# Retention's output projection as a one-level Strassen product in two parts of K

## The chip, the core and the metric

The kernel runs on one core of one Trainium2 chip. A core has a matrix engine (PE, TensorE), a vector engine (DVE), an activation engine (ACT), a general engine (POOL, GpSimd) and a queue that issues transfers (SP). Each engine carries out its own list of instructions in order and waits where an operand is not ready. The metric is the device time of one execution in microseconds. The median of three runs of the kernel before is 1336.56 us (1333.08 to 1337.13).

## The reference

One inference step of a two-layer trunk: a retention layer, then a sliding-window attention layer, for 1024 prompt tokens and 8 decode tokens of width 1024. What matters here is the end of the retention layer:

```python
    o, S = retention_scan(q, k, v, S0)
    o = rmsnorm(o, g_out.reshape(RET_HEADS, RET_DV)).reshape(B, L, RET_V)
    o = o * jax.nn.silu(gate)
    return x + o @ w_out, S.astype(S0.dtype)
```

There are 4 heads of 512 value columns, so `o` is tokens x 2048 and `w_out` is 2048 x 1024: the output projection has K = 2048, 1024 features and 1032 tokens. The attention layer then normalises the result `x + o @ w_out` and projects it to queries, keys, values and a gate. All values are float32.

## The kernel before

All projections are matmuls of 128x128 weights against up to 512 token columns. To keep float32 accuracy each operand is split into a rounded part ("hi", made by ACT or DVE) and a remainder ("lo", a subtraction on POOL or DVE), and each product is made of three matmuls: hi with hi, hi with lo, lo with hi.

The program has four stages on PE. *Input projection* (to about 546 us): q, k, v and the gate of the retention layer. Most of it is already a one-level Strassen product: `SEQ7` lists seven products of a weight combination (`A11`, `S1`, ...) with a token combination (`B11`, `T1`, ...), which take the place of eight. Its results go to DRAM. *Retention* (to about 700 us): 32 steps, each one chunk of 128 tokens of one head, heads 0 and 1 alternating through all 8 chunks, then heads 2 and 3. A step loads q, k, v and gate from DRAM, forms scores, updates the state, normalises, transposes the result to features x tokens (`b_tr`), multiplies it by the gate (`b_og`, DVE) and splits it: `b_oh` on ACT writes the hi part, `b_ol` on POOL (line 998) the lo part, into `A_hi`, `A_lo` (first 512 tokens) and `B_hi`, `B_lo` (the rest). *Output projection* (lines 1188 to 1190): for each of 8 feature tiles, 16 K tiles against 512 token columns, then again against 256 and 264. The first 24 matmuls (`e_mm`, lines 1026 to 1028) run before the last step's transposes. `wslot` loads and splits the weights 512 KB at a time, twice over, once for each half of the tokens. `ro_finish` adds the residual x by transposes into the same accumulator, writes the result to the DRAM buffer `xscr`, sums squares, and for the second half splits it at once into `A_hi`, `A_lo`; `reload2` brings the first half back. *Attention layer*: K/V projection (`kv_mm`, line 1338) from 901 us, then query and gate projections interleaved with attention (lines 1134 to 1136), then the last output projection.

In the input projection and the retention the order of every engine's work is written out by hand: PE has a list of slots, and the other engines' operations are placed by planned times or by slot (`when`, `later`) and then issued in that order. In the output projection PE's order is that of the loops, and the other engines' instructions are ordered by the compiler's scheduler.

## Time and profile before

| | us |
|---|---|
| median of three runs | 1336.56 |
| span of the profiled execution | 1336.3 |
| PE busy | 1293.8 (97%) |
| POOL busy | 832.5 (62%) |
| DVE busy | 743.8 (56%) |
| ACT busy | 668.4 (50%) |
| first matmul of the output projection | 700.49 |
| first matmul of the K/V projection | 901.01 |

Times in the profile are counted from the start of the profiled execution; its span is the profiled execution's own time, and lies 0.3 us under the median of the runs. A row of a timeline gives start, duration, engine, line, operation, output<-inputs and shape; in square brackets stands the idle time just before it and what ended that. PE's matmuls are pipelined: the duration of one is longer than its distance to the next, so costs are read from distances between starts. "PEclk" or "granted clock" is the share of PE's full clock that was granted.

### The profile page before, as it was taken

To read this page: it belongs to the slowest core of one execution; us is meant where nothing else is said; L and a number is where in the kernel's file an instruction comes from. 1 tells how busy PE (TensorE), PEld (TensorE's weight loads), DVE (VectorE), ACT (ScalarE), POOL (GpSimd) and SP (SyncE) were. 2 spreads that over 40 slices of the span, in tenths; PEclk is the share of its full clock that TensorE was granted. 3 is DMA by queue.
4 is the path that set the end of the run, shared out by engine and by line. 5 is a ranking of instruction groups with operands and counts; after the bars stand their busy time and mean duration, and the time that the engine had idled before them with its cause. 6 is when DMAs were issued, how large, how long until landed. Compare 5 with 4: busy or idle time off the path is not lost. (4 is left out here: it accounts for less than half of the span.)

```text
span 1336.3 us, 25984 instructions
## 1 busy us (share of the span) xinstructions
PE 1293.8 (97%) x9421; PEld 1233.6 (92%) x9421; DVE 743.8 (56%) x1497; ACT 668.4 (50%) x1692; POOL 832.5 (62%) x968
## 2 busy tenths in 40 slices
PE   6999999999999999898998999999999999999998
PEld 5999999999999999787886889999999999998998
DVE  6953665665565654477772212315677777778411
ACT  5532555555555653476771011235577666766321
POOL 6653556656556664398895654545688787868410
PEclk9999999999999999899998999999999999999999
DMA  6313767576666752656455634551131121103532
GB/s 223 103 58 118 241 189 248 157 243 213 195 211 215 231 174 83 191 161 218 158 165 164 188 110 136 155 151 47 58 95 48 33 60 33 48 20 116 176 95 76
DMA packets 193859, 187.18 MB, mean 140 GB/s; under 512 B 12756, under 2 KB 173580, under 8 KB 193716
## 3 DMA queue, kind: packets, MB, share of 16 engines
q1 hardware_dynamic: 160336, 153.19, 37.3%
q10 hardware_dynamic: 33396, 32.34, 7.7%
q8 instruction: 74, 1.21, 0.4%
q14 instruction: 53, 0.43, 0.1%
HBM read 129.11 MB, written 57.41 MB: 140 GB/s over the span
## 5 line engine op out<-in xcount | busy, mean ns | idle before, releaser
L340 PE MATMUL b<-xh,woh 128*128 128x258 f32 x784 | 222.2, 283 | 0.0
L342 PE MATMUL b<-xh,wol 128*128 128x258 f32 x784 | 221.7, 283 | 0.0
L341 PE MATMUL b<-xl,woh 128*128 128x258 f32 x784 | 221.4, 282 | 0.0
L1134 PE MATMUL pj<-A_hi,wh 128*128 128x384 f32 (+1 forms) x512 | 172.8, 337 | 0.0
L1135 PE MATMUL pj<-A_lo,wh 128*128 128x384 f32 (+1 forms) x512 | 164.6, 322 | 1.0 <-POOL A_lo L1489 0.7
L1136 PE MATMUL pj<-A_hi,wl 128*128 128x384 f32 (+1 forms) x512 | 164.3, 321 | 0.0
L340 PEld LDWEIGHTS b<-xh,woh 128*128 128x128 f32 x784 | 148.1, 189 | 1.2
L341 PEld LDWEIGHTS b<-xl,woh 128*128 128x128 f32 x784 | 148.7, 190 | 0.0
L342 PEld LDWEIGHTS b<-xh,wol 128*128 128x128 f32 x784 | 148.0, 189 | 0.0
L1124 POOL TENSOR_TENSOR wl<-wr,wh 128x1024 fp32r<-128x1024 f32 (+1 forms) x40 | 88.5, 2224 | 74.6 <-ACT wh L1121 37.8
L334 PE MATMUL b<-wol,xh 128*128 128x256 f32 x448 | 126.0, 281 | 1.2 <-DVE wol L224 1.2
L333 PE MATMUL b<-woh,xh 128*128 128x256 f32 x448 | 125.8, 281 | 0.0
L335 PE MATMUL b<-woh,xl 128*128 128x256 f32 x448 | 125.7, 281 | 0.0
L282 POOL TENSOR_TENSOR yl<-yd,yh 128x256 fp32r<-128x256 f32 x64 | 56.1, 876 | 79.6 <-PE od L289 40.3
L224 POOL TENSOR_TENSOR wol<-raw,woh 128x512 fp32r<-128x512 f32 x52 | 68.9, 1333 | 48.0 <-ACT woh L219 47.0
L1135 PEld LDWEIGHTS pj<-A_lo,wh 128*128 128x128 f32 x512 | 97.0, 189 | 1.6 <-POOL A_lo L1489 1.0
L1134 PEld LDWEIGHTS pj<-A_hi,wh 128*128 128x128 f32 x512 | 97.0, 189 | 0.6 <-issue 0.3
L1136 PEld LDWEIGHTS pj<-A_hi,wl 128*128 128x128 f32 x512 | 96.8, 189 | 0.0
L1688 POOL TENSOR_TENSOR s<-s,sm 128x512 f32<-128x512 f32 x64 | 66.6, 1040 | 34.0 <-DVE sm L1687 33.3
L334 PEld LDWEIGHTS b<-wol,xh 128*128 128x128 f32 x448 | 84.3, 188 | 1.4 <-DVE wol L224 1.4
L333 PEld LDWEIGHTS b<-woh,xh 128*128 128x128 f32 x448 | 84.3, 188 | 0.7
L335 PEld LDWEIGHTS b<-woh,xl 128*128 128x128 f32 x448 | 84.3, 188 | 0.0
(387 smaller groups left out, 3874.8 us busy)
## 6 DMA issues: line engine op xcount, KB each, us to landing
raw<-in_w_in_ret_dram ACTq DMA_DIRECT2D x44, 512.0 KB
st<-in_state_ret_dram SPq DMA_DIRECT2D x64, 256.0 KB
out_dram<-st SPq DMA_DIRECT2D x64, 256.0 KB
wr<-in_w_out_ret_dram SPq DMA_DIRECT2D x32, 512.0 KB
wr<-in_w_in_swa_dram SPq DMA_DIRECT2D x18, 512.0 KB
vb<-vscr SPq DMA_DIRECT2D x64, 128.0 KB
evp<-qks SPq DMA_DIRECT2D x32, 256.0 KB
evw<-gsc SPq DMA_DIRECT2D x32, 256.0 KB
```

The source lines that it names most:

```text
L224: eng.tensor_tensor(lo, src_of(s, name, sub), hi.bitcast(F32), SUB)
L333: mm(dst, xh, wh, start=a and i == 0, stop=False, skip_group_check=True)
L334: mm(dst, xh, wl, start=False, stop=False, skip_group_check=True)
L335: mm(dst, xl, wh, start=False, stop=z, skip_group_check=True)
L340: mm(dst, wh, xh, start=a, stop=False, **sg)
L341: mm(dst, wh, xl, start=False, stop=False, **sg)
L342: mm(dst, wl, xh, start=False, stop=z, **sg)
L1124: lo_eng[0].tensor_tensor(lo[:, js, :], raw[:, i:i + step, :], hi.bitcast(F32)[:, js, :], ALU.subtract)
L1134: mm(ps, hi[:, k, fs], xh[:, k, t0:t1], start=first and k == ks[0], stop=False)
L1135: mm(ps, hi[:, k, fs], xl[:, k, t0:t1], start=False, stop=False)
L1136: mm(ps, lo[:, k, fs], xh[:, k, t0:t1], start=False, stop=last and k == ks[-1])
L1688: nc.gpsimd.tensor_tensor(u.st[:, :, 0:256], u.st[:, :, 0:256], u.sm.unsqueeze(2).broadcast_to([128, 2, 256]), ALU.mult)
```

## The change

The output projection becomes a one-level Strassen product, made twice: once for the first half of K (heads 0 and 1) and once for the second (heads 2 and 3). Within a part, K is halved between the two heads, the features within a group of 256 are halved, and tokens are halved into even and odd chunks. There are 2 x 4 sets (part, group of 256 features), each of seven products in the order of `SEQ7`, each product in two slots (`t`, halves of the tokens) of 4 K tiles x 3 matmuls of 258 columns (256 prompt tokens and 2 decode tokens).

- Operands of part one: `b_og` writes the gated result of heads 0 and 1 into 16 held tiles (`hold`); `plan_builds` places the splits and the sums of five of the seven operands in steps 6 to 30 of the retention. The other two, T3 and T4, are split when the retention's tiles have been released (`late_build`). `b_oh`, `b_ol` and `e_mm` are gone.
- Operands of part two: `b_og` of heads 2 and 3 goes to DRAM (`osc`), is loaded again during sets 1 to 3 for the sums (`tsum`), stored, and all seven operands are loaded and split during the fourth set (`xb_load`, `xb_build`), through five buffers (`ob_load`).
- Partial results of part one, with the residual, go to DRAM (`pasc`), and are added in part two (`pa_load`, `pa_add`, `o_evac`). Weights are loaded once, and their sums formed on POOL (`w_sum`).
- The finished result goes to `xscr` and, except for the last 256 features, is loaded and split again (`a_load`, `a_split`) during the last set and at the start of the K/V projection, which now takes the odd chunks first (`KORD`).
- The whole kernel up to the last projection is now ordered by hand. The table `Table` has one slot of 1.45 us for each half product (0.23 more where residual transposes follow); its slots run from 0 to 169.8 us, the eight sets begin at 0, 22.1, 44.3, 66.4, 88.6, 108.9, 129.2 and 149.5, and the other engines' work is placed by these times.

The attention layer keeps its matmuls and their order after the K/V projection; its weight tiles are cut into pieces of another size.

```diff
+    osc = [dp.tile([8, 2, 128, 4, 128 + 2 * m], F32, name=f"osc{m}") for m in range(2)]
+    pasc = dp.tile([4, 4, 128, 516], F32, name="pasc")
...
-    A_hi = ap.tile([128, 8, NT], F32R, name="A_hi")
-    A_lo = ap.tile([128, 8, NT], F32R, name="A_lo")
-    A_hif = A_hi.bitcast(F32)
-    p2 = ExitStack()
-    bp = p2.enter_context(tc.tile_pool(name="bp", bufs=1, side="right", reuse_waits="tile"))
-    B_hi = bp.tile([128, 16, 520], F32R, name="B_hi")
-    B_lo = bp.tile([128, 16, 520], F32R, name="B_lo")
...
+    hold = {(h, c): ho.tile([128, 4, 128], F32, tag=f"h{h}{c}", name="hold") for h in range(2) for c in range(NCH)}
...
+    def xo_alloc(x):
+        pool_, n = (xb[0], 4) if x in (T3, T4) else (xo, 10)
+        OX[x] = [pool_.tile([128, 4, 2, 258], F32R, tag="xo", bufs=n, name=nm) for nm in ("oxh", "oxl")]
...
+    def ox_hi(x, j, src):
+        act(ox_cs(x, j, src.shape[2])[0], src, AF.Copy)
+
+    def ox_lo(x, j, src, eng=pool):
+        h, l = ox_cs(x, j, src.shape[2])
+        eng.tensor_tensor(l, src, h.bitcast(F32), SUB)
...
+        og = hold[h, c] if h < 2 else rp.tile([128, 4, 128], F32, name="og", bufs=2)
+        dve.tensor_tensor(og, d.pop(("pt", c)).rearrange("p (i t) -> p i t", i=4), d.pop(("g", c)), MUL)
+        if h >= 2:
+            ogs.append((osc[c // 2 % 2][(0, 2, 1, 3)[2 * (h % 2) + c % 2], c // 4][:, :, 0:128], og))
...
-    def e_mm():
-        ps = ro_ps[0, 0] = trp.tile([128, 512], F32, name="tr")
-        xh, xl, _ = o_view(0)
...
+    def plan_builds(first, last):
+        seq_ = []
+        for j in range(4):
+            a_, c_ = hold[0, 2 * j], hold[0, 2 * j + 1]
+            b_, d_ = hold[1, 2 * j], hold[1, 2 * j + 1]
+            for x, y in ((B11, a_), (B21, b_), (B22, d_)):
+                seq_ += [(ox_hi, x, j, y), (ox_lo, x, j, y)]
+            seq_ += [(sum_op, a_, c_, a_), (sum_op, c_, d_, c_), (ox_hi, T1, j, a_), (ox_lo, T1, j, a_),
+                     (sum_op, d_, d_, a_), (ox_hi, T2, j, d_), (ox_lo, T2, j, d_), (sum_op, b_, b_, d_)]
+        for n_, x in enumerate(seq_):
+            j = n_ * 4 // len(seq_)
+            builds.setdefault(max(4 * j + 6, first + n_ * (last - first) // len(seq_)), []).append(x)
+
+    plan_builds(6, 30)
...
+    def ob_load(n_, j):
+        y = ob[0].tile([128, 4, 128 + 2 * (j % 2)], F32, tag="ob", bufs=5, name="ob")
+        nc.sync.dma_start(out=y, in_=osc[j % 2][n_, j // 2])
+        return y
...
+    def o_product(s, ps, t, name, x, first, res):
+        hi, lo = s.op[name, 0]
+        dst = ps[:, 0:258]
+        for k in range(4):
+            wh, wl = hi[:, k, :], lo[:, k, :]
+            xh, xl = OX[x][0][:, k, t, :], OX[x][1][:, k, t, :]
+            a, z = first and k == 0, k == 3 and res is None
+            sg_k = dict(skip_group_check=not first)
+            mm(dst, wh, xh, start=a, stop=False, **sg_k)
+            mm(dst, wh, xl, start=False, stop=False, **sg_k)
+            mm(dst, wl, xh, start=False, stop=z, **sg_k)
+        if res is not None:
+            for i in range(2):
+                nc.tensor.matmul(ps[:, 128 * i:128 * i + 128], res[:, 2 * t + i, :], ident, is_transpose=True,
+                                 start=False, stop=(i == 1), skip_group_check=not first)
...
+    def o_raw(s, j):
+        t = s.pool().tile([128, 4, 256], F32, tag="raw", bufs=2, name="raw")
+        nc.sync.dma_start(out=t, in_=w_out_ret[1024 * s.part + 512 * j:1024 * s.part + 512 * j + 512, s.c0:s.c0 + 256]
+                          .rearrange("(k p) f -> p k f", p=128))
+        s.raw.append(t)
...
+        elif j == 3 and s.part == 0:
+            act(o_out(s, "c", t), b0, AF.Copy)
+        elif j == 3:
+            dve.tensor_tensor(o_out(s, "c", t), b0, s.pa["c"][:, t, :], ADD)
+        elif j == 4 and s.part and s.q:
+            dve.tensor_tensor(c["w", t], b1, c["w", t], ADD)
...
+    def out_a(s, key, i, par):
+        dc = both(s, key)[:, :, 256:258]
+        ft = 2 * s.q + i
+        pool.tensor_tensor(dc, dc, xd[:, ft, dsl(par)].rearrange("p (t c) -> p t c", t=2), ADD)
+        soon_dma(pasc[s.q, "cwxp".index(key)], s.full[key])
...
+        if s.q == 3:
+            if AT[3] is None:
+                at_alloc(3)
+            ahi, alo, af = [y[:, i, 0:NP].rearrange("p (t c r x) -> r p t c x", r=2, c=2, x=128)[par]
+                            for y in (*AT[3], AT[3][0].bitcast(F32))]
+            act(ahi, pr, AF.Copy, scale=gk)
+            dve.scalar_tensor_tensor(alo, pr, gk, af, MUL, SUB)
...
+    def a_split(k, par):
+        g = a_st.pop((k, par))
+        if AT[k // 2] is None:
+            at_alloc(k // 2)
+        gk = gcol[:, 16 + k:17 + k]
+        ahi, alo = [a_par(y[:, k % 2], par) for y in AT[k // 2]]
+        act(ahi, g, AF.Copy, scale=gk)
+        dve.scalar_tensor_tensor(alo, g, gk, ahi.bitcast(F32), MUL, SUB)
...
+        res = s.part == 0 and j >= 3
+
+        def pe():
+            if first:
+                s.bk[b, t] = o_bank(b, t)
+            o_product(s, s.bk[b, t], t, name, x, first, s.res[KEYS[j - 3][0]] if res else None)
+
+        tb.slot(1.45 + (0.23 if res else 0.0), pe)
+        tb.later(n + 1, o_evac, s, j, t)
...
+            th_ = max(tf - 6.5, floor + (3.2 if name != "A11" else 0.0))
+            tl_ = th_ + 1.4
...
+            tb.when(max(min(reads) - 15.0 + 0.5 * j, 10.0 if s is osets[1] else -1e9), o_raw, s, j)
...
+    def tsum(j):
+        a_, b_, c_, d_ = t_st.pop(j)
+        for eng, out, x, y, n_ in ((dve, a_, c_, a_, 4), (pool, c_, d_, c_, 6), (dve, d_, d_, a_, 5), (pool, b_, b_, d_, 7)):
+            eng.tensor_tensor(out, x, y, SUB)
+            soon_dma(osc[j % 2][n_, j // 2], out, 2)
...
+    def xb_build(x, j):
+        y = x_st.pop((x, j))
+        if j == 0:
+            xo_alloc(x)
+        ox_hi(x, j, y)
+        ox_lo(x, j, y, (dve, pool)[j % 2])
...
+    for n_, (x, j) in enumerate([(x, j) for x in (T3, T4) for j in range(4)]):
+        tb.when(4.5 + 0.6 * n_, late_build, x, j)
...
+        tb.when(13.0 + 12.3 * j, tsum_load, j)
+        tb.when(19.5 + 12.3 * j, tsum, j)
+    m = 0.0
+    for n_, x in enumerate(ORD7):
+        for j in range(4):
+            m = max(m + 1.1, osets[3].t0 + 2.95 * n_ + 3.0)
+            tb.when(m - 6.0, xb_load, x, j)
+            tb.when(m, xb_build, x, j)
...
+    for k in range(6):
+        m = e7 + 3.1 + 2.0 * k
+        tb.when(m - 5.0, a_load, k, 1)
+        tb.when(m, a_split, k, 1)
+    for k in range(2):
+        tb.when(e7 + 11.0 + k, a_load, k, 0)
+        tb.when(e7 + 15.6 + 2.0 * k, a_split, k, 0)
...
+    tb.pe()
+    others(len(steps))
+    store_s()
+    tb.rest()
+    for _ in range(2):
+        tb.pe()
+        if tb.n == 2:
+            at_step(b_tr, len(steps) - 1)
+        tb.rest()
+    others(len(steps) + 1)
+    store_s()
+    open_b()
...
-    npool = 0
-    for ft in range(8):
-        if ft:
-            drain(ro_part(ft, 0, 0, ps2 if npool % 3 else pjp))
-        npool += 1
-        drain(ro_part(ft, 0, 1, None))
-        ro_finish(ft, 0)
...
+    KORD = (1, 3, 5, 7, 0, 2, 4, 6, 8)
...
+    for k in range(2, 6):
+        a_load(k, 0, lambda: atp.tile([128, 4, 128], F32, tag="qs", bufs=4, name="ar"))
...
```

The order of the instructions shows the change at three places. First PE at the end of the retention. Before, the last early matmuls of the projection (`eh`, `el`: early weights) are followed by the transposes of the last step (`on`) and by the rest of the first tile (`wh`, `wl`: weights from `wslot`):

```order
L1028 MATMUL tr_9799<-A_hi_7711,el_7723 128x512
L1026 MATMUL tr_9799<-A_hi_7711,eh_7722 128x512
L1027 MATMUL tr_9799<-A_lo_7712,eh_7722 128x512
L1028 MATMUL tr_9799<-A_hi_7711,el_7723 128x512
L103 MATMUL tr_9824<-ident_69,on_9789 128x128 x4
L1188 MATMUL tr_9799<-A_hi_7711,wh_9860 128x512
L1189 MATMUL tr_9799<-A_lo_7712,wh_9860 128x512
L1190 MATMUL tr_9799<-A_hi_7711,wl_9861 128x512
```

Now the same transposes stand inside the second product (`oxh`, `oxl`: a token operand, `woh`, `wol`: a weight operand, `S`: an accumulator that held the state), between its two halves:

```order
L1127 MATMUL S_9885<-oxh_7739,woh_9818 128x258
L1128 MATMUL S_9885<-oxl_7740,woh_9818 128x258
L1129 MATMUL S_9885<-oxh_7739,wol_9819 128x258
L104 MATMUL tr_9898<-ident_71,on_9856 128x128 x4
L1127 MATMUL S_9919<-oxh_7739,woh_9818 128x258
L1128 MATMUL S_9919<-oxl_7740,woh_9818 128x258
L1129 MATMUL S_9919<-oxh_7739,wol_9819 128x258
```

The matmuls that stood ahead of the last transposes needed two 256 KB weight tiles; three slots of products stand there now.

Second, ACT in the middle of the projection. Before, it has the evacuation of a tile (`x`), its square and its store:

```order
L1213 ACTIVATE x_10070<-pj 128x256
L1213 ACTIVATE x_10076<-pj 128x256
L1221 ACTIVATE sq<-x_10070 128x256
L1223 DMA xscr<-x_10070 128x256
L1221 ACTIVATE sq<-x_10076 128x256
L1223 DMA xscr<-x_10076 128x256
```

Now, in the fourth set, the reloaded blocks (`ob`) are converted between the weight conversions (`woh`) and the evacuations (`evp`) of the sets:

```order
L881 ACTIVATE oxh_11062<-ob_11011 128x4x128
L881 ACTIVATE oxh_11139<-ob_11037 128x4x128
L238 ACTIVATE woh_11145<-s1_11007 128x512
L881 ACTIVATE oxh_11139<-ob_11060 128x4x130
L881 ACTIVATE oxh_11139<-ob_11066 128x4x128
L1148 ACTIVATE evp_11185<-S_11150 128x258
L881 ACTIVATE oxh_11139<-ob_11089 128x4x130
L238 ACTIVATE woh_11192<-raw_10789 128x512
```

The weights of a set and its evacuations have come to stand behind blocks that wait for DRAM. Third, SP's queue in the projection. Before, weights (`wr`) and residuals (`xr`):

```order
L1116 DMA wr<-in_w_out_ret_dram 128x4x256 x4
L1200 DMA xr<-in_x_prompt_dram 128x4x128
L1116 DMA wr<-in_w_out_ret_dram 128x4x256 x4
L1200 DMA xr<-in_x_prompt_dram 128x4x128
L1116 DMA wr<-in_w_out_ret_dram 128x4x256 x2
```

Now, in the fourth set, the reloads (`ob`) with weights (`raw`) and stores of partial results (`pasc`) among them:

```order
L1112 DMA ob<-osc_68 128x512
L1136 DMA pasc<-evc 128x516
L1112 DMA ob<-osc_69 128x520
L1140 DMA raw<-in_w_out_ret_dram 128x4x256 x2
L1112 DMA ob<-osc_68 128x512
L1112 DMA ob<-osc_69 128x520
L1136 DMA pasc<-evw 128x516
```

The weights of the next set stand behind reloads, each of which waits for one of five buffers.

698 lines of the change are left out of this document (449 added, 249 removed).

## The prediction

> **What bounds the kernel now.** I began with the page's busy times and its chain of waits, to learn which engine ends the program.
>
> ```profile
> span 1336.3 us, 25984 instructions
> PE 1293.8 (97%) x9421; PEld 1233.6 (92%) x9421; DVE 743.8 (56%) x1497; ACT 668.4 (50%) x1692; POOL 832.5 (62%) x968
> PE pj L1134 4%; PE pj L1135 4%; PE pj L1136 4%; PE pj L1188 4%; PE pj L1189 4%; PE pj L1190 4%; PE tr L103 2%; POOL s L1688 1%; POOL wl L1106 1%; PE sc L1667 1%; PE sc L1668 1%; PE pm L1559 1%; PE o L1718 1%; PE o L1716 1%; POOL gt L1599 1%
> ```
>
> TensorE is busy 97% of the span, and the output projection of the retention layer (L1188 to L1190) is 12% of the span on the chain. The averages hide stages, so next come the windows around the projection (columns: length, busy time and count of PE, PEld, DVE, ACT, POOL, granted clock, DMA share, GB/s).
>
> ```profile
> 550.00:560.00 10.00, 6.52 (x34) 5.33 (x33) 5.53 (x12) 6.37 (x15) 5.70 (x8) 0.85 0.98 323
> 580.00:600.00 20.00, 20.00 (x110) 16.89 (x109) 15.90 (x38) 15.10 (x37) 18.62 (x23) 1.00 0.52 170
> 700.00:710.00 10.00, 7.12 (x34) 5.17 (x32) 4.26 (x6) 3.33 (x7) 2.94 (x4) 1.00 0.55 197
> 710.00:720.00 10.00, 7.00 (x21) 5.11 (x22) 2.20 (x5) 0.00 (x0) 7.24 (x4) 0.66 0.59 175
> 820.00:860.00 40.00, 40.00 (x335) 39.53 (x334) 13.32 (x18) 7.61 (x20) 22.73 (x15) 1.00 0.45 133
> ```
>
> Retention (580 to 600) already keeps PE full, with POOL close behind at 18.62 of 20. The steady projection (820 to 860) is PE alone. Only the passage from one to the other (700 to 720) is poor: PE idles and the granted clock falls to 0.66. The timeline shows why.
>
> ```profile
> 700.49 0.48 PE L1026 MATMUL tr<-A_hi,eh 128*128 128x512 f32 x1
> 707.25 0.60 PE L103 MATMUL tr<-ident,on 128*128 128x128 f32 x4
> 711.42 0.80 PE L1188 MATMUL tr<-A_hi,wh 128*128 128x512 f32 x1 [3.57 <-DVE wh L1123]
> 714.23 0.80 PE L1190 MATMUL tr<-A_hi,wl 128*128 128x512 f32 x1 [1.58 <-POOL wl L1124]
> 901.01 0.37 PE L1338 MATMUL pj<-wh,A_hi 128*128 128x256 f32 x1
> ```
>
> The early matmuls begin at 700.49, PE waits 3.57 and 1.58 us for split weights, and the K/V projection takes over at 901.01. So the projection holds PE from 700.49 to 901.01: **200.5 us**, the amount to be replaced.
>
> **PE's new work.** The change issues 8 sets of 7 products x 2 token halves x 4 K tiles x 3 terms = 1344 matmuls of 258 columns, instead of 384 of 512 and 768 of 256 or 264. The input projection already runs that shape; two of its rows, 72 matmuls apart, give the pitch, and the chain of waits gives one 512-wide tile (48 matmuls and 4 residual transposes).
>
> ```profile
> 537.83 0.28 PE L342 MATMUL b<-xh,wol 128*128 128x258 f32 x1
> ...
> 546.50 0.28 PE L342 MATMUL b<-xh,wol 128*128 128x258 f32 x1
> ```
> ```profile
> 721.07 0.44 PE tr L103 x4
> 732.67 0.44 PE pj L103 x4
> ```
>
> The pitch is (546.50 - 537.83) / 72 = 120.4 ns, so 1344 cost 161.8 us. The 64 residual transposes cost 0.44 / 4 = 0.11 each, 7.0 in all; the last transposes of the retention, now inside the projection, 0.6 (row at 707.25), and the eight small ones of x_sample at most 0.5. New PE time **169.9**: 30.6 less than 200.5. Half of that is arithmetic and half the passage: the old matmuls needed 384 x 0.2325 = 89.3 us (732.67 - 721.07 - 0.44 = 11.16 over 48) and 768 x 119.4 ns = 91.7 (40 us / 335, transposes included), with about 4 for the first half's transposes 185 of the 200.5.
>
> [...]
>
> **The passage.** The first weights and operands are now formed during the retention, and the last transposes come after three product slots, so PE should not wait there. What may wait is the fifth product: T3 and T4 are built after the retention's tiles close, eight conversions on ACT and eight subtractions. The engines' prices, for this and what follows:
>
> ```profile
> L219 ACT ACTIVATE woh<-s 128x512 fp32r<-128x512 f32 x88 | 54.3, 622 | 28.2 <-PE b L334 8.7 <-POOL s L203 8.4 <-POOL s L209 5.2
> L224 DVE TENSOR_TENSOR wol<-s,woh 128x512 fp32r<-128x512 f32 x88 | 69.8, 799 | 4.8 <-ACT woh L219 3.9
> L224 POOL TENSOR_TENSOR wol<-raw,woh 128x512 fp32r<-128x512 f32 x52 | 68.9, 1333 | 48.0 <-ACT woh L219 47.0 <-DMA raw<-in_w_in_ret_dram 0.8
> L203 POOL TENSOR_TENSOR s<-s,raw 128x512 f32<-128x512 f32 x22 | 30.6, 1389 | 0.6
> L998 POOL TENSOR_TENSOR A_lo<-og,A_hi 128x512 fp32r<-128x512 f32 x16 | 20.6, 1284 | 0.0
> L994 ACT ACTIVATE A_hi<-og 128x512 fp32r<-128x512 f32 x16 | 10.2, 639 | 0.0
> ```
>
> Planned from 4.5 us on, T3's four conversions take 4 x 0.62 = 2.5 and the last subtraction 1.3, ready near 8.3 against a need at 12.1 us; T4's, which reuse tiles of the state stores, have until 18.8. Bounds 0 to 3, taken 0.5.
>
> **Retention.** It loses 32 subtractions on POOL (32 x 1.28 = 41 us) and 32 conversions on ACT, and gains 20 of each plus 16 subtractions on DVE (16 x 0.80 = 12.8) between steps 6 and 30. DVE goes from 15.9 of 20 us by about 2.3 (0.53 per 4.5 us step) to 18.2, still under PE. The added stores, 16 x 256 KB on SP behind the loads, add some 58 GB/s (4.2 MB in 16 steps) to 170, under the 323 seen above. PE covers all of it and pays nothing; relieving POOL returns nothing, because PE is full. If DVE's cover failed, its next product, `on`, would be late for PE's transposes. Bounds -2 to +3, taken 0.
>
> **Engines within a set.** Over the 20 to 22 us of a set ACT has 7 x 0.62 plus four evacuations, DVE 7 x 0.80 plus ten, POOL 4 x 1.39 and a few additions: half loads or a little more, as in the input projection, where the same order of products leaves PE full.
>
> **The reload is the weak place.** In the fourth set (66.4 to 88.6 us after the first product by the table of slots, 1.45 us a slot and 0.23 more with a residual) the 28 operand blocks of the second K half come back through DRAM: 256 KB each, loaded 6.0 us ahead, converted every 1.1 us from 69.4 to 99.1, through five buffers. Products need them from 88.6 (B11) to 107.4 (last half of T4). One such load, and POOL's spread:
>
> ```profile
> 834.18 3.37 SPq L1229 DMA_DIRECT2D wr<-xscr  x2
> 836.82 0.72 ACT L1230 ACTIVATE A_hi<-wr,gcol 128x512 fp32r<-128x512 f32 x1 [8.58 <-DMA wr<-xscr]
> L224 POOL TENSOR_TENSOR wol<-raw,woh x9: 1283/1296/1751, 303.3 to 390.9; 128x512 fp32r<-128x512 f32 x9
> ```
>
> A load lands in 2.64 us. A buffer's round is then 2.64 + 0.62 + 1.33 + about 0.4 for the issue = 5.0, over five buffers 1.0 us a block: just inside 1.1. But the traffic planned from 60 to 95 us is 7.3 MB of reloads, 2.1 of weights, 1.1 of residuals and 2.6 of partial results, 13.1 MB: 375 GB/s, where the busiest window (share 0.98) moved 323. It takes 40.6 us instead of 35 and ends 5.6 us late. POOL has 14 x 1.33 + 6 sums x 1.39 + a difference = 28.4 us of work in those 30, or 37 at the slowest 1.75. The weights' conversions of the fifth set stand behind the blocks in ACT's queue and so do SP's stores, so all slip together. Against it stands a lead of 6.5 us before each product, less 0.62 and 0.80: 5.1. Best case no stall; lags of 5.6 and 7 added, less 5.1, give 7.5; with longer rounds more (below). Taken 3, nearer the first lag alone, since the two mostly overlap.
>
> [...]
>
> **Entering the K/V projection.** Half of A is read back during the last set; four blocks (even chunks, feature tiles 2 to 5) are loaded only once the last product has freed their space. K/V starts on odd chunks and wants the first two after seven half tiles of 12 matmuls, about 10 us; load 2.6, issues 1.2 and splits fit. Extra ACT and DVE work there (four splits of 0.72 on ACT and 0.80 on DVE, decode columns) can delay the norms. Bounds -1 to 6, taken 1.5. The second layer keeps its matmuls and their order: 0.
>
> **Sum.** 1336.3 - 30.6 + 0.5 + 0 + 3 + 1.5 = 1310.7, **1311 us**. The profiled execution's span of 1336.3 lies 0.3 under the median of the runs (1336.56), so nothing is added.
>
> **Rivals.**
> - *Reload rounds lengthen.* If loads under this traffic take 6.5 us instead of 2.64, the round is 8.9, the block 1.77, and the last is done at 69.4 + 27 x 1.77 + 2 = 119.2 instead of 107.4: 11.8 late, 1305.7 + 11.8 + 2 = **1320** (1316 to 1332). For it: 375 against 323. Against: less traffic after 95 lets it catch up.
> - *The same chain, slower than before.* Place: five buffers, SP waiting in order for each. It decides where a load takes 10.4 us, four times the row above: blocks every 2.55 us, the last at 140, 33 late. At 11 us it gives **1344**. Against: the old projection kept PE full (820 to 860) on loads twice that size.
> - *K/V entry.* The read-back waits for the last product, PE goes idle and the clock drops as at 710: 6 to 10 us, **1317**.
> - *The width buys nothing*, a matmul costing the same whatever its columns: (89.3 + 91.7) / 1152 = 0.157 us each, 1344 of them 211, with 8.1 of transposes 18.6 more than 200.5: **1355**. The shape's own 120.4 ns all but excludes it. [...]
>
> **How the numbers follow.** Forecast (1302 to 1316) 0.62; longer rounds 0.22; K/V entry 0.05; the same chain beyond 10 us 0.07; no gain for other reasons 0.03; width 0.01. The range of 80% leaves out only the tail of the longer rounds and the slow cases: 1302 (no stall at all, and retention 2 us better) to 1325. A difference under 0.3%, about 4 us and as much as the three runs differ among themselves, is no change: faster 0.89, same 0.03, slower 0.08.
>
> **What would show it.** Right: PE without a gap at the end of the retention; matmuls of 258 columns 120 ns apart; about 170 to 175 us from the first product to the first K/V matmul; retention steps still 4.5 us. The weak place would show as waits of ACT on reloaded blocks, and of PE on ACT, some 85 to 110 us after the first product, at a DMA share near 1. The prediction is wrong if PE idles over 8 us there, if the clock falls in any set, or if retention steps lengthen because DVE is late.

## The result and the profile after

The changed kernel takes 1337.76 us (median of 20 runs) against 1335.86 for the kernel before (20 runs): a ratio of 1.0015 (95% interval 1.0005 to 1.0025). The forecast was 1311. The 30.6 us that PE should have saved were spent elsewhere.

The first rows of the page after, and the row of a window from 700 to 1000 us, first before and then after (length, busy time and count of PE, PEld, DVE, ACT, POOL, granted clock, DMA share, GB/s):

```profile
span 1335.1 us, 26918 instructions
PE 1276.3 (96%) x9613; PEld 1231.1 (92%) x9613; DVE 852.9 (64%) x1684; ACT 709.0 (53%) x1739; POOL 852.9 (64%) x1011
```
```profile
700.00:1000.00 300.00, 293.69 (x1965) 270.77 (x1963) 109.50 (x235) 98.57 (x287) 175.30 (x157) 0.99 0.40 123
```
```profile
700.00:1000.00 300.00, 282.58 (x2184) 275.30 (x2183) 205.12 (x397) 145.97 (x351) 207.53 (x214) 0.99 0.58 182
```

PE's busy time fell by 17.5 us over the program, but DVE's busy time between 700 and 1000 us nearly doubled, from 109.5 to 205.1 us, and PE is no longer full there. The timeline gives the ends of the stages: the first transposes of the retention, and a late mark in the attention (transposes of scores, `s`, for which PE waits on POOL), before and after; in the kernel after also the first matmul of sets 1, 4, 5, 6, 7 and 8 and of the K/V projection.

```profile
547.34 0.68 PE L863 MATMUL tr<-evp 128*128 128x128 f32 x4 [0.57 <-issue]
1000.93 0.66 PE L103 MATMUL tr<-ident,s 128*128 128x128 f32 x4 [1.36 <-POOL s L1688]
```
```profile
549.57 0.68 PE L913 MATMUL tr<-evp 128*128 128x128 f32 x4 [0.56 <-issue]
708.29 0.36 PE L1127 MATMUL S<-oxh,woh 128*128 128x258 f32 x1
777.85 0.36 PE L1127 MATMUL S<-oxh,woh 128*128 128x258 f32 x1
800.71 0.36 PE L1127 MATMUL S<-oxh,woh 128*128 128x258 f32 x1
829.52 0.28 PE L1127 MATMUL S<-oxh,woh 128*128 128x258 f32 x1
849.71 0.28 PE L1127 MATMUL S<-oxh,woh 128*128 128x258 f32 x1
870.16 0.28 PE L1127 MATMUL S<-oxh,woh 128*128 128x258 f32 x1
894.01 0.28 PE L1687 MATMUL pj<-pw,A_hi 128*128 128x256 f32 x1
1001.75 0.66 PE L104 MATMUL tr<-ident,s 128*128 128x128 f32 x4 [1.32 <-POOL s L2038]
```

| us, profiled executions | before | by the prediction | after |
|---|---|---|---|
| input projection | 547.3 | 547.3 | 549.6 |
| retention, to the first matmul of the projection | 153.2 | 153.2 | 158.7 |
| output projection | 200.5 | 173.4 | 185.7 |
| K/V projection and start of the attention, to the mark | 99.9 | 101.4 | 107.7 |
| the rest | 335.4 | 335.4 | 333.4 |
| span | 1336.3 | 1310.7 | 1335.1 |

The expectations below call that mark the first scores. The first transposes of scores stand earlier, at 950.68 before and 951.47 after, with the same difference of 7.8 us from the first K/V matmul.

A span is 1.7 to 2.4 us shorter (mostly 1.8) than the device time of its execution, wherever the record has both; it is not that execution's own time, as was said ahead of the prediction. The execution profiled after took 1336.95 us, 0.8 under the median of its kernel; the one profiled before must, by the same difference, have taken some 1338.1, 2.2 over the median of its own. So the spans miss the forecast change of -25.6 us by 24.4, and the medians miss it by 27.5.

The matmuls do what was forecast: the sixth set has no residuals and no wait, and (849.71 - 829.52) / 168 is 120.2 ns. Most of the rest is waits. Three things carry them.

**Retention: DVE.** Between 630 and 675 us DVE was busy 33.2 us before and 39.6 after:

```profile
630.00:675.00 45.00, 41.73 (x221) 35.19 (x221) 33.18 (x75) 31.55 (x75) 38.24 (x46) 0.96 0.57 193
```
```profile
630.00:675.00 45.00, 37.35 (x203) 30.29 (x202) 39.56 (x90) 28.15 (x68) 35.02 (x41) 1.00 0.75 221
```

The groups of DVE's instructions in this window that are new (busy time, mean ns), and two of PE's waits in it:

```profile
L1052 DVE TENSOR_TENSOR hold<-hold 128x512 f32<-128x512 f32 x6 | 4.2, 699 | 0.0
L896 DVE TENSOR_TENSOR oxl<-gdec,oxh 128x16 fp32r<-128x16 f32 x5 | 2.8, 551 | 0.2
L901 DVE TENSOR_TENSOR gdec<-gdec 128x16 f32<-128x16 f32 x4 | 2.3, 570 | 0.1
L895 DVE CAST oxh<-gdec 128x16 fp32r<-128x16 f32 x5 | 1.7, 335 | 0.0
```
```profile
637.11 0.63 PE L104 MATMUL tr<-ident,on 128*128 128x128 f32 x4 [1.82 <-DVE on L1025]
658.51 0.63 PE L104 MATMUL tr<-ident,on 128*128 128x128 f32 x4 [1.93 <-DVE on L1025]
```

The operations on 16 decode columns take 6.8 us, more than the sums of 128x512 beside them (4.2). Their size is not what makes them long. At the K/V entry, with POOL idle, a subtraction of 16 columns takes 0.17 us; in the retention it meets an instruction of POOL that began 0.1 us earlier, and ends with it:

```profile
638.25 0.74 POOL L962 TENSOR_TENSOR ql<-evp,qh 128x256 fp32r<-128x256 f32 x1
638.35 0.67 DVE L896 TENSOR_TENSOR oxl<-gdec,oxh 128x16 fp32r<-128x16 f32 x1
```
```profile
912.85 0.17 DVE L1262 TENSOR_TENSOR A_lo<-odT,A_hi 128x16 fp32r<-128x16 f32 x1
```

**DVE is slower beside POOL.** In the last set, DVE's subtraction of 128x512 takes 1.78 us, where the same took 0.69 with POOL idle:

```profile
738.19 0.69 DVE L243 TENSOR_TENSOR wol<-s,woh 128x512 fp32r<-128x512 f32 x1
```
```profile
888.61 1.78 DVE L243 TENSOR_TENSOR wol<-raw,woh 128x512 fp32r<-128x512 f32 x1
890.31 0.41 DVE L1158 TENSOR_TENSOR evw<-S,evw 128x258 f32<-128x258 f32 x1
```
```profile
888.51 1.33 POOL L1228 TENSOR_TENSOR acc<-acc,sq 128x516 f32<-128x516 f32 x1 [1.11 <-ACT sq L1227]
889.78 1.75 POOL L1195 TENSOR_TENSOR evp<-evp,pa 128x516 f32<-128x516 f32 x1
```

POOL's sum began 0.1 us earlier and ended at 889.84; DVE's subtraction ended 0.55 later, where it takes 0.69 with POOL idle, and POOL's next one took 1.75, where the same line took 1.29 at 849.06 with DVE idle. The evacuation behind it, which reads the accumulator and one tile, takes 0.41. Between 700 and 900 us, the 16 subtractions of 128x512 on DVE during which POOL did nothing took 0.67 to 0.69 us each, and the 62 that met an instruction of POOL 0.67 to 1.80.

**The clock falls in steps.** PE's longest wait is in the fifth set. ACT waits for a reloaded block, DVE for ACT, and the weight that PE needs stands behind them (`wol`), as the order had it; SP had stood at six reloads for 10.68 us before (the first and last conversions of blocks are shown with it):

```profile
793.56 10.68 SPq L1112 DMA_DIRECT2D ob<-osc  x6
```
```profile
781.69 1.15 ACT L881 ACTIVATE oxh<-ob 128x512 fp32r<-128x512 f32 x2
...
813.61 0.63 ACT L881 ACTIVATE oxh<-ob 128x512 fp32r<-128x512 f32 x1 [2.48 <-DMA ob<-osc]
...
823.46 0.64 ACT L881 ACTIVATE oxh<-ob 128x520 fp32r<-128x520 f32 x1 [0.70 <-DMA ob<-osc]
```
```profile
814.27 0.69 DVE L885 TENSOR_TENSOR oxl<-ob,oxh 128x512 fp32r<-128x512 f32 x1 [5.69 <-ACT oxh L881]
814.88 0.68 DVE L243 TENSOR_TENSOR wol<-raw,woh 128x512 fp32r<-128x512 f32 x1
```
```profile
815.62 0.58 PE L1129 MATMUL S<-oxh,wol 128*128 128x258 f32 x1 [3.84 <-DVE wol L243]
```
```profile
811.00:814.00 3.00, 0.78 (x7) 0.57 (x5) 0.00 (x0) 0.52 (x2) 2.11 (x2) 1.00 1.05 401
814.50:821.00 6.50, 5.38 (x25) 5.38 (x26) 6.31 (x10) 3.91 (x8) 5.88 (x4) 0.50 0.93 295
```

The clock fell 1.2 us before the end of the wait of 3.84 us and stood at one half for 6.8 us. "Lost clock" below is this loss: each half microsecond times one minus its granted clock, added over a stretch; here it is 3.4 us. In almost every stretch of every profile it comes in steps of 1.7 us, and the same wait has it in one execution and not in the next; the last section shows when.

### The profile page after: what moved, and what is told of

Its sections match the earlier page's. It is cut to its first block, busy times and chain, and to the rows that moved or that the text cites. A ratio compares the mean times of both kernels' runs of the same rounds, so it can differ in the third digit from the quotient of the medians.

```text
span 1335.1 us, 26918 instructions
## 1 busy us (share of the span) xinstructions
PE 1276.3 (96%) x9613; PEld 1231.1 (92%) x9613; DVE 852.9 (64%) x1684; ACT 709.0 (53%) x1739; POOL 852.9 (64%) x1011
## 4 chain that ended last, share of the span: by engine, by line
PE 67%; POOL 11%; DVE 10%; DMA 6%; issue 4%; ACT 2%; SPq 0%; POOLq 0%; ACTq 0%; DVEq 0%
PE b L359 7%; PE b L361 7%; PE b L360 7%; PE pj L1593 5%; PE pj L1594 5%; PE pj L1595 5%; PE b L353 4%; PE b L354 4%; PE b L352 4%; PE tr L104 3%; DMA ob<-osc 2%; DVE Sl L1006 1%; POOL s L2038 1%; POOL pw L1578 1%; PE S L1129 1%
## 5 line engine op out<-in xcount | busy, mean ns | idle before, releaser
L1593 PE MATMUL pj<-A_hi,pw 128*128 128x384 f32 (+1 forms) x512 | 172.5, 337 | 0.0
L1594 PE MATMUL pj<-A_lo,pw 128*128 128x384 f32 (+1 forms) x512 | 163.9, 320 | 1.0 <-POOL A_lo L1840 0.7
L1595 PE MATMUL pj<-A_hi,pw 128*128 128x384 f32 (+1 forms) x512 | 163.8, 320 | 0.0
L361 PEld LDWEIGHTS b<-xh,wol 128*128 128x128 f32 x784 | 148.0, 189 | 0.0
L243 DVE TENSOR_TENSOR wol<-s,woh 128x512 fp32r<-128x512 f32 x120 | 102.0, 855 | 18.3 <-ACT woh L238 17.6
L238 ACT ACTIVATE woh<-s 128x512 fp32r<-128x512 f32 x120 | 73.9, 623 | 71.2 <-POOL s L212 32.4
L243 POOL TENSOR_TENSOR wol<-raw,woh 128x512 fp32r<-128x512 f32 x52 | 68.9, 1332 | 52.1 <-ACT woh L238 51.2
L1594 PEld LDWEIGHTS pj<-A_lo,pw 128*128 128x128 f32 x512 | 96.6, 189 | 1.6 <-POOL A_lo L1840 1.0
L1127 PE MATMUL S<-oxh,woh 128*128 128x258 f32 x320 | 94.2, 294 | 3.8 <-DVE evw L1158 2.8
L1593 PEld LDWEIGHTS pj<-A_hi,pw 128*128 128x128 f32 x512 | 96.4, 188 | 0.6 <-issue 0.3
L1595 PEld LDWEIGHTS pj<-A_hi,pw 128*128 128x128 f32 x512 | 96.2, 188 | 0.0
L1129 PE MATMUL S<-oxh,wol 128*128 128x258 f32 x320 | 92.0, 287 | 3.8 <-DVE wol L243 3.8
L1128 PE MATMUL S<-oxl,woh 128*128 128x258 f32 x320 | 91.5, 286 | 0.0
```

The lines of the kernel that those rows point to most:

```text
L243: eng.tensor_tensor(lo, src_of(s, name, sub), hi.bitcast(F32), SUB)
L361: mm(dst, wl, xh, start=False, stop=z, **sg)
L1127: mm(dst, wh, xh, start=a, stop=False, **sg_k)
L1129: mm(dst, wl, xh, start=False, stop=z, **sg_k)
L1593: mm(ps, wh, AH(k)[:, t0:t1], start=first and k == ks[0], stop=False)
L1594: mm(ps, wh, AL(k)[:, t0:t1], start=False, stop=False)
```

## Experiments

"Net" is a stretch without its lost clock. The profiles of the kernels below show how far a stretch varies that an edit did not touch: retention net 155.0 to 157.8 us (nine profiles, middle 156.4), sets 1 to 3 net 69.4 to 71.7 (middle 70.9), sets 4 and 5 net 48.3 to 51.2 (nine, middle 49.7).

For whole programs the record has more than the profiles: span and granted clock of every execution. Span times clock, averaged over a kernel's executions, is called the program's net below, and the rest of the span its lost clock. In the kernel before the net is the same whenever it was run (means of 1324.8, 1325.1, 1324.9 and 1324.8 over 26, 31, 31 and 7 executions). In the kernel after it is 1326.6 (20 executions), with 9.6 us of lost clock. The standard error of a mean of 10 executions is 0.4 to 0.8 us.

### The reload

Three theories for the fourth and fifth set (51.7 us against 42.2 of matmuls and residuals): the buffer's round, the bytes, the subtractions.

```diff
-        x_st[x, j] = ob_load({B11: 0, B21: 1, B22: 3, T1: 4, T2: 5, T3: 6, T4: 7}[x], j)
+        if not one:
+            one.append(ob_load(0, 1))
+        x_st[x, j] = one[0] if j % 2 else one[0][:, :, 0:128]
```


> Leaves out the loads of the second K half in the fourth set: one block is loaded and all 28 conversions read it (so every operand of part two is made of the same block), with the same conversions and subtractions. In the changed kernel the fourth and fifth sets took 22.9 and 28.8 us, where 22.0 and 20.3 are matmuls. Theory 1 (the round of a buffer: landing, conversion, subtraction, over five buffers) and theory 2 (landing under traffic alone) both expect these two sets to fall from 51.7 to 44 us or less and the program to be 6 to 9 us faster than the changed kernel, about 1329. Theory 3 (the subtractions on DVE and POOL hold each other up, loads or not) expects them to stay at 48 or more and the program within 3 us of the changed kernel.

Measured: 1333.33 us (ratio to before 0.998, 0.9965 to 0.9995), 4.4 under the changed kernel. The two sets took 46.8 us, 45.5 net. So the loads cost about 4 us net, less than theories 1 and 2 said, and another 3 us over the matmuls remain with no load at all. The program's net fell by 3.1.

```diff
-        x_st[x, j] = ob_load({B11: 0, B21: 1, B22: 3, T1: 4, T2: 5, T3: 6, T4: 7}[x], j)
+        n_ = {B11: 0, B21: 1, B22: 3, T1: 4, T2: 5, T3: 6, T4: 7}[x]
+        y = ob[0].tile([128, 4, 128 + 2 * (j % 2)], F32, tag="ob", bufs=5, name="ob")
+        nc.sync.dma_start(out=y[:, 0:1], in_=osc[j % 2][n_, j // 2][:, 0:1])
+        x_st[x, j] = y[:, 0:1].broadcast_to([128, 4, 128 + 2 * (j % 2)])
```


> Keeps all 28 loads, the five buffers and every wait, but each load brings a quarter of its block (64 KB), and the conversions read this quarter four times over. Theory 2 (bytes: landing under traffic) expects nearly all of the gain of the kernel with one block, 5 to 9 us, since a landing falls from about 4.6 us to the 2 us of an undisturbed one. Theory 1 expects a part of it, 3 to 6 us, because the conversion and the subtraction remain in the round. Theory 3 expects under 2 us.

Measured: the two sets 46.9 us with no lost clock, about 3 less net than with whole blocks; the program 1337.93 (ratio 1.0018, 0.9999 to 1.0036), no gain, though its net fell by 1.9. In the profiled execution a residual that landed late cost PE 2.1 us in the first set.

```diff
-        ox_lo(x, j, y, (dve, pool)[j % 2])
+        ox_lo(x, j, y, dve)
```


> All 28 subtractions of the reloaded blocks on DVE instead of 14 on DVE and 14 on POOL. DVE's subtraction of 128x512 takes 0.67 us where POOL is idle and up to 1.78 where POOL is subtracting, POOL's takes 1.2 to 1.75. Theory 3 and theory 1 expect the fourth and fifth sets to become 4 to 8 us shorter: 14 x 1.25 us leave POOL, 14 x 0.67 come to DVE, and a buffer is released earlier. Theory 2 expects no change over 1.5 us, or a loss of up to 2 because DVE has more to do.

Measured: the two sets 50.2 us, 46.8 net; the wait for `wol` fell to 2.3 us, but one for a residual rose to 2.2. The program took 1339.8 (1.0017, 1.0002 to 1.0031), and its net rose by 1.1: what the two sets gained was not a gain of the program.

```diff
-        y = ob[0].tile([128, 4, 128 + 2 * (j % 2)], F32, tag="ob", bufs=5, name="ob")
+        y = ob[0].tile([128, 4, 128 + 2 * (j % 2)], F32, tag="ob", bufs=4, name="ob")
...
```


> Four buffers for the reloaded blocks instead of five, everything else unchanged (the first loads, for the sums, use the same buffers in fours). Theory 1: the blocks came every 1.5 us over five buffers, a round of 7.5 us, so over four they come every 1.9, the last is 10 us later, and the program 6 to 12 us slower than the changed kernel. Theories 2 and 3 expect under 3 us, since bytes and subtractions remain the same.

> Six buffers for the reloaded blocks instead of five (a table of constants that the attention needs moves to a place that is opened later). Four buffers had made the fourth and fifth sets 2.9 us longer than the profiled run of five, and the third 3.0; no loads at all made the fourth and fifth 4.9 shorter. Theory 1 (the round of a buffer) expects the fourth and fifth sets at 47.5 to 50 us instead of 51.7. Theories 2 and 3 expect no change over 1 us.

Measured with four buffers: 1345.31 us (1.0062, 1.0029 to 1.0095), 7.5 over the changed kernel as theory 1 expected of the whole; but the two sets lengthened only to 54.6 (50.6 net), and sets 1 to 3, whose sums use the same buffers, took 73.1 (72.0 net, against a middle of 70.9). With six: 1335.87 (0.9989, 0.9976 to 1.0002), the two sets 49.1 with no lost clock, inside what untouched kernels show. So none of the three theories is right alone: by one profile each, bytes and the subtractions are worth about 3 us net in these sets (whether the two add up was not tried); a sixth buffer, taken alone, is worth 1 us or less there.

### The retention

```diff
     def sum_op(out, x, y):
-        dve.tensor_tensor(out, x, y, SUB)
+        pass
```


> Leaves out the 16 sums of 128x512 on DVE in the retention (the operands T1 to T4 of part one are then built from unsummed blocks). In the changed kernel the retention, from its first transposes to the first product of the projection, took 158.7 us, where the kernel before needed 153.2 to its first projection matmul, and PE waited 12.0 us for the product `on` of DVE. Theory A (DVE is full: 39.6 of 45 us between 630 and 675, against 33.2 before): without the sums, 0.7 us each, the late steps shorten, and the retention falls by 2 to 4 us. Theory B (the queue of loads, now mixed with 16 stores of 256 KB, is late): under 1 us.


```diff
-        dve.tensor_copy(h, src)
-        dve.tensor_tensor(l, src, h.bitcast(F32), SUB)
+        act(h, src, AF.Copy)
+        act(l, src, AF.Copy)
...
     def dec_sums():
+        return
```


> Leaves out the subtractions and sums of the decode columns in the retention (16 columns each, steps 17 to 22): their high and low parts are both plain copies on ACT, so the decode columns of part one are wrong. On DVE these small operations took 6.8 us between 630 and 675, more than the sums of 128x512 there (4.2). Theory A expects the retention to fall by 2 to 4 us, with the waits from 632 to 670 smaller or gone. Theory B expects under 1 us.

> Leaves out both, the 16 sums and the decode columns' work on DVE. Theory A expects the retention back at 153 to 154 us, as before the change, and the program 5 to 6 us faster than the changed kernel, near 1332. Theory B expects the retention above 157 and no gain over 1.5 us.


```diff
-        dve.tensor_copy(h, src)
-        dve.tensor_tensor(l, src, h.bitcast(F32), SUB)
+        act(h, src, AF.Copy)
+        pool.tensor_tensor(l, src, h.bitcast(F32), SUB)
...
-            dve.tensor_tensor(out, x, y, SUB)
+            pool.tensor_tensor(out, x, y, SUB)
```


> Computes the same. The small operations on decode columns in the retention leave DVE: the copies go to ACT, the subtractions and sums to POOL. Leaving them out on DVE (with POOL doing nothing for them) had shortened the retention from 158.7 to 157.9 us, leaving the sums out to 155.3, both to 149.2. Theory A (time on DVE) expects 157 to 158. The rival (POOL and DVE exclude each other, so that work moved to POOL still costs DVE) expects 158.5 or more.


```diff
-            dve.tensor_copy(d["qh", c], d["l", c][0][:, 0:2, :])
+            act(d["qh", c], d["l", c][0][:, 0:2, :], AF.Copy)
```


> Computes the same: the decode columns and the copies of q in the retention off DVE, nothing else. One look, for the retention alone: theory A expects 150 to 152 us from the first transposes to the first product, the rival (ACT or POOL is late in its turn) 153 or more.

| retention | us | lost clock | net |
|---|---|---|---|
| before | 153.2 | 5.1 | 148.0 |
| after | 158.7 | 1.7 | 157.0 |
| without the sums | 155.3 | 3.4 | 151.9 |
| without the decode work | 157.9 | 5.1 | 152.8 |
| without both | 149.2 | 0.0 | 149.2 |
| decode work on ACT and POOL | 153.2 | 0.0 | 153.2 |
| the same, and q's copies on ACT | 154.4 | 1.7 | 152.7 |

Theory A holds: against the middle of 156.4 the sums cost 4.5 us and the decode work 3.6, without both all but 1.2 of the loss is gone, and the stores, which all these kernels keep, are not its cause. The decode work on ACT and POOL cost PE next to nothing, less than theory A said, which speaks against the rival of the fourth kernel. Moving the 28 copies of q as well gained 0.5, no more than can be told, and missed what was expected. The program's time moved less: 1334.82 (ratio 0.9985, 0.9972 to 0.9998), 1337.35 (1.0005, 0.9989 to 1.0020), 1335.77 (0.9982, 0.9966 to 0.9999) and 1337.06 (1.0005, 0.9990 to 1.0020) for the first four, one run of 1336.33 for the fifth. The program's net shows where the gain is. It fell by 3.9, 3.1, 5.3 and 2.3 us in the first four kernels, not far from the 4.5, 3.6, 7.2 and 3.2 by which the retention's net stands under its middle; but they lost 10.3, 12.2, 11.9 and 11.0 us of clock instead of 9.6, which took part of it away again. Without both, the retention was 9.5 us shorter than in the profile after and the projection behind it 4.8 longer (190.5), with waits of 2.1 and 1.9 us for residuals in sets 3 and 4; the projection of other kernels with the changed order took 185.7 to 188.8, so a part was given back there as well.

### The sums of part two

```diff
-        for eng, out, x, y, n_ in ((dve, a_, c_, a_, 4), (pool, c_, d_, c_, 6), (dve, d_, d_, a_, 5), (pool, b_, b_, d_, 7)):
+        for eng, out, x, y, n_ in ((dve, a_, c_, a_, 4), (dve, c_, d_, c_, 6), (dve, d_, d_, a_, 5), (dve, b_, b_, d_, 7)):
```


> The four sums of each quarter of part two, formed in sets 1 to 3, alternate between DVE and POOL and depend on one another; here all four are on DVE, with the same result. In the changed kernel POOL stood idle for 18.8 us in sets 1 to 3 before these sums and DVE for 12.3 us (6.5 of them for the loads), and PE waited 1.0 and 0.7 us (2.1 and 1.2 in another run) for residuals that POOL makes behind them. Theory S (the in-order engines hold each other up at these sums) expects the waits of PE for residuals in the third and fourth set to go, and sets 1 to 4, 92.4 us, to come to 89 to 90. The rival (the residual's own load is late) expects them to stay within 1 us.

POOL's waits between 708 and 780 us of the kernel after (total, times, longest):

```profile
POOL ob L1354 <- DVE ob L1354: 10.6, 5, 5.6
POOL ob L1354 <- DMA xr<-in_x_prompt_dram: 8.2, 2, 7.4
```

With the sums on DVE these rows are gone. The third set's wait for a residual went, the fourth's stayed at 0.8; sets 1 to 3 took 68.7 us, under the 69.4 to 71.7 of untouched kernels, and sets 1 to 4 91.7. So theory S is right about the third set and gained less than it said (89 to 90). The program took 1337.32 (1.0003, 0.9989 to 1.0017).

### The last set and the K/V projection

```diff
-            tb.later(n + (2 if (s.part, s.q) != (1, 3) else 1), out_b if s.part else out_a, ...)
+            tb.later(n + 2, out_b if s.part else out_a, ...)
```


> In the last set alone, the finishing of a result (conversion on ACT, subtraction on DVE, decode columns, square) is issued one slot later, as in the other sets, so that the evacuation of the next product stands ahead of it in DVE's queue. In each run of the changed order PE waited 2.8 us there for DVE's evacuation, and the set took 23.9 to 25.2 us for 20.3 us of matmuls. Theory E (the evacuation stands behind a subtraction that waits for ACT) expects the wait to fall to 1.5 us or less and the set by 1.5 to 3. The rival (DVE's subtractions, lengthened to 1.8 us by POOL, fill the time) expects the wait to stay above 2.3.

PE's wait in the last set, after and with this edit:

```profile
890.87 0.36 PE L1127 MATMUL S<-oxh,woh 128*128 128x258 f32 x1 [2.80 <-DVE evw L1158]
```
```profile
890.17 0.36 PE L1127 MATMUL S<-oxh,woh 128*128 128x258 f32 x1 [1.61 <-DVE evw L1158]
```

The wait fell by 1.2 us, a little short of what was expected; the set took 22.6 us instead of 23.9 in the profile after and 24.9 to 25.2 in most others, 1.7 of which was lost clock, and lost none. What is left of the wait fits the rival: in this profile a subtraction of 1.46 us, beside POOL, and one of 0.74 stand ahead of the evacuation. The program took 1336.24 (0.9998, 0.9985 to 1.0011).

```diff
-        if n == 3:
+        if n == 2:
             rstd9(0)
...
-        if n == 2:
-            a_dec()
...
         if n == 4:
+            a_dec()
```


> Computes the same. At the entry of the K/V projection the norms of the even chunks are issued one step earlier, ahead of the last four splits of A, and the eight small splits of the decode columns two steps later. In the changed kernel PE waited there 2.2 us for the norms and 1.0 us for a key, both behind two splits and the decode splits in DVE's queue. Theory D (order in DVE's queue) expects these waits to shrink from 3.2 to under 1 us and the stretch from the first K/V matmul to the first scores, 107.7 us, to fall by 2 to 4. The rival (POOL's short powers, 0.7 us each in a chain with DVE, set the pace) expects the stretch to stay within 1 us.

After, DVE had two late splits of A and nine decode operations ahead of the norms (`r`), and PE waited:

```profile
910.11 2.36 DVE L1253 SCALAR_TENSOR_TENSOR A_lo<-ar,gcol,A_hi 128x512 fp32r<-128x512 f32 x2
...
913.82 0.15 DVE L1618 TENSOR_SCALAR r<-tr 128x4 f32<-128x4 f32 x1
```
```profile
914.37 0.41 PE L104 MATMUL tr<-ident,kd 128*128 128x128 f32 x2 [2.18 <-DVE r L1618]
917.23 0.36 PE L1687 MATMUL sc<-pw,A_hi 128*128 128x256 f32 x1 [1.02 <-DVE kd L1668]
```

With the norms first, this wait was gone, but two others stood there, 0.98 (`kd`) and 0.67 (a split of the keys). The stretch was 105.5 us; kernels with the old order had 105.7 to 107.7, of which up to 3.5 was lost clock, so the gain was not resolved. The program took 1338.46 (1.0009, 0.9993 to 1.0025). Before the change the stretch took 99.9 us and PE stood idle for none of it; in the profile after it stood idle for 5.7 us, and here still for 3.4.

### The edits together

> Computes the same, with five edits together: decode columns of the retention off DVE, part-two sums all on DVE, six buffers for the reload, the last set's finishing one slot later, the norms of the even chunks one step earlier. One at a time they shortened their own stretch: 3.2 us (retention, with the clock's share taken out), 2.9 (third set), 0.7, 2.5 and 2.0. Theory W (five separate waits, each in its own place) expects the sum, 8 to 11 us under the changed kernel, about 1328. The rival (a wait removed in one place is given back in the next, as the retention's 9 us were where the sums and decode columns were left out and the projection became 4.8 longer) expects 1332 to 1337.

> The five edits and two more: all subtractions of the reload on DVE (which made the fourth and fifth sets 1.5 us shorter when tried alone, but PE's wait for a residual 1.5 longer), and the copies of q in the retention on ACT instead of DVE (32 x 0.28 us). Theory A (DVE is what is late in the retention) expects the retention at 150 to 152 us, below the 153.2 that the kernel with the decode columns off DVE had, and the program 2 to 4 us under the five edits. The rival expects no gain over them.

The five edits (decode work off DVE, the sums of part two on DVE, six buffers, `out_b` one slot later, norms first) take 1323.71 us: a ratio to before of 0.9908 (0.9893 to 0.9922). With the subtractions of the reload on DVE and q's copies on ACT it is 1320.19: 0.9880 (0.9864 to 0.9897). Both do the whole computation, and both beat the kernel before, by 0.9 and 1.2%. The intervals overlap, so what the last two edits add is not settled; the retention with them took 153.6 us (151.9 net), above what theory A expected. The marks of the five edits, for sets 1 to 6 and K/V:

```profile
703.99 0.37 PE L1127 MATMUL S<-oxh,woh 128*128 128x258 f32 x1
728.11 0.37 PE L1127 MATMUL S<-oxh,woh 128*128 128x258 f32 x1
750.06 0.37 PE L1127 MATMUL S<-oxh,woh 128*128 128x258 f32 x1
772.02 0.37 PE L1127 MATMUL S<-oxh,woh 128*128 128x258 f32 x1
793.99 0.37 PE L1127 MATMUL S<-oxh,woh 128*128 128x258 f32 x1
818.78 0.28 PE L1127 MATMUL S<-oxh,woh 128*128 128x258 f32 x1
...
882.26 0.28 PE L1687 MATMUL pj<-pw,A_hi 128*128 128x256 f32 x1
```

Sets 2 to 4 are now 21.95, 21.96 and 21.97 us, the price of their matmuls and residuals; the fifth is 24.8 and the projection 178.3 instead of 185.7, without lost clock. The retention is 157.2 (153.8 net) and K/V to the mark in the attention 104.8. The rival expected 1332 to 1337 and is refuted. The time fell by more than theory W said (14.0 against 8 to 11). One at a time the medians of the five edits stand between 1.9 us under and 0.7 over the changed kernel's and sum to -3.8, so the five seem to be worth more together than alone. The means over all executions show why:

| kernel | executions | span | lost clock | net |
|---|---|---|---|---|
| before | 31 | 1334.6 | 9.6 | 1324.9 |
| after | 20 | 1336.3 | 9.6 | 1326.6 |
| decode work off DVE | 10 | 1335.3 | 11.0 | 1324.3 |
| sums of part two on DVE | 10 | 1334.9 | 9.9 | 1325.0 |
| six buffers | 10 | 1332.8 | 8.3 | 1324.6 |
| `out_b` one slot later | 10 | 1334.4 | 9.2 | 1325.2 |
| norms first | 10 | 1336.1 | 9.1 | 1327.0 |
| the five edits | 4 | 1321.5 | 4.0 | 1317.5 |
| the seven edits | 4 | 1318.9 | 4.6 | 1314.3 |

Net of the clock the single edits sum to -7.0 (standard error about 3), and together they give -9.1: within that they simply add up, and theory W's 8 to 11 is right for this part. The other 5.6 us are clock. All four executions of the five edits lost 1.3 to 5.3 us of it, those of the kernel after 4.0 to 16.1. Stage by stage the profile tells the same: against the middle of untouched stretches the five edits gain net 2.6 in the retention, 2.9 in sets 1 to 3, 2.9 in sets 4 and 5, some 0.7 in the last set and 0 to 2 in K/V, about 10; and from the first product to the mark it has no lost clock and no wait of PE over 1.6 us, where the kernel after has waits of 3.84, 2.80 and 2.18. A kernel with one edit keeps the other waits. That the waits' end is why the clock fell less rests on that one profile and on what the last section shows of waits and clock. No kernel reached the forecast of 1311: the seven edits end 9 us above it.

## Why the prediction was wrong, point by point

- *PE's new work, 169.9 us*: right. The pitch was 120.2 ns against 120.4, and sets with no wait took what was priced. The rival that width buys nothing, at 157 ns a matmul, is refuted.
- *The passage, 0.5*: right in that PE no longer waits for weights there and loses no clock. But its neighbour was missed: the sums of part two in sets 1 to 3 were not priced at all. Sets 1 to 3 took 69.6 us, 2.9 more than 3 x 22.0 and 0.6 for the last transposes.
- *Retention, "PE covers all of it and pays nothing"*: the step that failed first. It came to 5.5 us, and to 8 to 9 net of the clock. The sum left out the operations on the decode columns (6.8 us on DVE in 45), and from a mean of 15.9 of 20 it concluded that DVE fits. In its place the runs showed PE waiting 12.0 us for `on`, the sums costing 4.5 us net and the decode work 3.6. The stage had less room than was read: "PE full" came from one window of 20 us, and over the whole stage PE had waited 5.5 us for `on` before the change, and was busy for 41.73 of 45 us from 630 to 675. The failure was named correctly, `on` late for the transposes, but bounded by 3.
- *"Engines within a set: half loads or a little more"*: wrong, and as far as the edits show the root of much of the rest. The durations were those of engines that get their operands at once. DVE ran at 205 of 300 us between 700 and 1000, its subtractions took up to 1.8 us beside POOL's where 0.80 was priced, and what counts in an in-order queue was what stands ahead. A mean load hides that. It shows in the waits for residuals, in the last set (23.9 us against 20.2, priced at nothing) and in part in the K/V projection. Edits that change only which engine does a step, or its place in a queue, took some 2 us off sets 1 to 3 and 1 off the last set.
- *The reload, taken 3*: the place and the chain (ACT on blocks, PE on ACT's queue, DMA share near 1, 85 to 110 us after the first product) were right, the size was not: sets 4 and 5 came to 9.5 over the matmuls, 6.1 of it net (7.5 by the middle of nine profiles). With no loads 3 of those remained. Blocks came about every 1.5 us, (823.46 - 781.69) / 27, between the planned 1.1 and the rival's 1.77.
- *K/V entry, 1.5*: 7.8 us longer than before, over the bound of 6. The cause that was named, splits ahead of the norms, is there, but it accounts for 3.2 of the 5.7 us that PE stood idle, and with the norms first the stretch was still 5.6 longer than before. No run isolates what makes the rest; some 2 us of it are not idle time of PE at all.
- *The rivals* were taken as alternatives. Longer reload rounds and the K/V entry happened at once, each in part, and with them what was no rival at all: 5.5 in the retention, 12.3 in the projection, 6.3 in K/V (over the terms taken), 2.2 in the input projection (the same order; other profiles had 546.7 to 549.6) and -2.0 in the rest give 24.3 of the 24.4 by which the span missed the forecast. The upper end of the rival of longer rounds, 1332, with the upper bounds of the retention (3) and of K/V (6, for the 1.5 taken) added, is 1339.5, and would have held the time; that is hindsight, since the loads alone came to about 4 and not to 11.8.

## What to carry to other kernels

This change took work from the busiest engine, gave it to three others and moved the bound to the waits between in-order queues (3.84, 2.80 and 2.18 us the longest after the first product), and these added up over the stages: price each place where an engine stands in front of another, and sum them. Count the small operations, and price DVE beside a working POOL at the length with waiting: up to 1.8 us here instead of 0.7 for 512 columns, and a mean of 0.55 instead of 0.17 for 16. When repairs alone seem to do nothing, take the lost clock out before judging them: net of it five edits summed to -7.0 alone and gave -9.1 together, and with the long waits gone the lost clock fell as well, from 9.6 to 4.0 us.

## What the runs showed of the hardware

- The granted clock fell on a grid. In each of the 17 profiles the falls to 0.50 begin whole multiples of 3.413 us apart (after: at 73.76, 561.87 and 814.45 us, 143 and 74 steps), and up to the last microseconds they last 3.41 us or 2 to 4 times that. So each cost 1.7 us or a multiple; the profiled executions lost 3.4 to 14.4 us in this way.
- Falls went with the time that PE stood idle within one step of the grid (its length less PE's busy time). Between 690 and 1000 us of the 17 profiles, 36 steps at full clock were followed by a fall, and each held at least 1.92 us of idle PE; the other 1468 held 1.86 at most, and none was followed by one. (This is not the whole of it: before, the fall at 1277.22 us follows a step in which PE was busy for all 3.41 us.) The wait of 2.80 us in the last set is the example. After, a step ends in its middle and leaves 1.47 and 1.33 us on either side, and the clock stays (columns as in the windows above):

```profile
886.13:889.54 3.41, 1.94 (x17) 1.73 (x15) 2.62 (x4) 1.86 (x3) 1.35 (x3) 1.00 1.02 309
889.54:892.96 3.42, 2.09 (x16) 2.00 (x17) 2.88 (x4) 0.51 (x1) 2.18 (x3) 1.00 0.33 98
```

With the sums of part two on DVE the same wait lies within one step, 2.80 us of it, and the clock is halved in the next:

```profile
884.78:888.19 3.41, 0.61 (x5) 0.43 (x4) 3.08 (x4) 1.43 (x3) 2.51 (x2) 1.00 0.85 244
888.19:891.60 3.41, 3.41 (x17) 3.41 (x17) 2.23 (x4) 1.86 (x3) 1.35 (x3) 0.50 0.25 77
```

- So PE's wait of 2.8 us cost up to 1.6 times its length (2.8 + 1.7). The one of 3.84 cost about 1.7 times its length, since 1.2 of its 6.8 us at half clock lay within it. A whole stage differed by this: the last set took 23.9 us in the profile after and 24.9 to 25.2, 1.7 of it lost clock, in most others.
